# Two-layer encoder trunk: maxima exchanged behind the second transposes, edge pairs and norm sums placed later, last projection tile loaded four k-tiles at a time

## The chip, the cores and the metric

The kernel runs on one core of one Trainium2 chip. The metric is device time in microseconds of one execution; the kernel before has a median of 1507.74 us over 3 runs (1507.51 to 1507.95). PE is TensorE, DVE is VectorE, ACT is ScalarE, POOL is GpSimd and SP is SyncE, which issues nearly all DMAs. A "bank" is one of the eight 128x512 fp32 tiles of PSUM that the program allocates.

## What is computed

Input x is 1x512x1024 in fp32. Two layers, each a token mixer and an MLP, both behind an RMS norm and both added to the stream:

```python
h = h + mixer_a(rms_norm(h, norm1[0]), a_wqkv, q_gain, k_gain, a_wo, cos, sin)   # layer 0
h = h + mlp_sq_relu(rms_norm(h, norm2[0]), mlp_w1[0], mlp_w2[0])
h = h + mixer_b(rms_norm(h, norm1[1]), b_win, b_conv, b_wout)                    # layer 1
h = h + mlp_sq_relu(rms_norm(h, norm2[1]), mlp_w1[1], mlp_w2[1])
```

`mixer_a` is windowed attention of 16 heads of 64 columns in three groups (dilations 1, 4 and 16), each with its own q, k and v; q and k are normalised per head and partly rotated. The three groups share one softmax: their row maxima are compared, each group is weighted by exp(own maximum - greatest maximum), and numerators and denominators are added. `mixer_b` is a gated three-tap convolution between two projections. `mlp_sq_relu` is relu(h @ w1) squared, @ w2, with 4096 hidden columns.

## The kernel before

Every large product is three matmuls in fp32r: each fp32 operand is split into a high part and the rest (`wh`, `wl` for weights, `hgh`, `hgl` for activations), and high x high, high x rest and rest x high are added in PSUM (`add_unit`, matmul at L128). `split` (L288, L289) makes the parts: ACT casts the high one, DVE or, for weights, POOL subtracts for the rest.

The work of TensorE is a list of units in a fixed order: for each of the eight head pairs the columns q0, k0, q1 (unit A), k1, q2, k2 (unit B) and v; then the attention's output projection `wo`, the MLP, the convolution mixer and the second MLP. A position counts unit size: 1.0 is 16 matmuls of 384 columns or 12 of 512 columns. Everything else is a task with a position, held in a heap; `run_tasks` issues a task's instructions, on whatever engines, as soon as the matmul before its position has been issued. So an engine's order is set by the positions, and an instruction that waits holds up all behind it on its engine. `PLACES` has three sets of positions: for the first pair, for pairs 1 to 6, and for the last.

Weights come through `load_to` (DMA issue on SP into one of four `wraw` buffers) and `prep_to` (cast on ACT into `wh`, difference on POOL into `wl`, six buffers each), one k-tile of 128 rows at a time.

The pieces of a head pair, in their order (`attn_tasks`):

- The evacuations to `rawA` or `rawB`, the squares (`norm_sq`, L362), the inverse root (`norm_rs`, twelve small DVE instructions from L365 on: L151, L152, then three times L155 to L157) and the multiplication with the rotation (`norm_mul`, to L378).
- TA and TB: the first and second transposes (`qk_fill`, L387): four transposes of 128x128 fill a bank, ACT takes the high part from it (L401) and DVE the rest (L403). TA makes q0, k0, q1; TB makes k1, q2, k2.
- S0: scores of group 0 in two halves (L443), two banks each; DVE adds the mask and takes the maxima (L447). E0: the exponentials.
- X: the exchange of maxima. Group 0 has another row order than groups 1 and 2, so its maxima and sums are permuted: `spread` (L424, DVE), then at X + lX `stats_over`, which is `swap` (four small matmuls into one bank, L433) and a copy out of it (L478, DVE).
- S12: scores of groups 1 and 2 in four pieces (L457, one bank each, maxima L460), E12 their exponentials, W the weights of the groups (a second `swap`, copy L496), N0 and N12 the normalisation (L504 on DVE, L502 on POOL).
- PT: eight transposes of the probabilities (L516), split into `pth` and `ptl`; PV: the products with v (L544).

Banks: the projections take theirs from a pool of four (`psG`), the outputs have one (`psO`). TA, TB, S0, S12, `swap` and PT all take theirs in turn from one pool of three (`psT`), so each waits until the use three before it has been read out. `ident` is the identity matrix, the moving operand of a transpose.

After the last pair the output projection adds `xs` back (a DMA fetches it to `oT`, L768; L739 adds). `add_sums` has the sum of squares for the next norm split (`sgh`, `sgl`) and summed over the partitions by two matmuls with ones (L711, L712), and DVE then works out the inverse root `R` from it (L714 on).

The change touches `PLACES`, `add_unit` (a factor for its size), `add_sums`, and the unit of the last 128 columns of `wo` (L779).

Of the kernel before, what the change touches and what calls it, by code (L numbers as in the profile page):

```python
# [35 lines left out]
def _constants():  # L36
# [10 lines left out]
    for n, b in enumerate((0, 1, 3)):  # L47
# [10 lines left out]


PLACES = [  # L60
    dict(sqA=0.52, rsA=0.95, mulA=2.62, dmA=0.05, TA=6.3, dT=0.2, sqB=0.08, rsB=1.22, mulB=2.1, dmB=0.1, TB=6.2, S0=1.25,
         dS=0.65, E0=2.4, X=4.2, lX=1.3, S12=7.8, dS12=0.3, E12=8.4, dE12=0.2, W=10.0, lW=0.35, lF=0.9, N0=11.35, N12=10.45,
         dN=0.04, P=12.2, dP=0.6, gP=0.5, lP=1.6, qA=0, qB=0, pA=0, pB=3, pN=2, vA=0, vB=8, xq=2.7, dxq=0.3, xs=5.35,
         lg=2.48, dlg=0.36, tb=4.6, dtb=0.15, gc=6.7),
    dict(sqA=0.02, rsA=0.87, mulA=1.79, dmA=0.28, TA=4.8, dT=0.19, sqB=0.17, rsB=0.8, mulB=1.07, dmB=0.12, TB=4.05, S0=0.45,
         dS=0.55, E0=1.1, X=3.1, lX=1.3, S12=6.5, dS12=0.24, E12=7.1, dE12=0.2, W=8.9, lW=0.35, lF=0.9, N0=10.25, N12=9.4,
         dN=0.04, P=10.9, dP=0.64, gP=0.9, lP=1.6, qA=0, qB=0, pA=0, pB=3, pN=2, vA=0, vB=12),
    dict(sqA=0.02, rsA=0.87, mulA=1.79, dmA=0.28, TA=4.8, dT=0.19, sqB=0.17, rsB=0.8, mulB=1.07, dmB=0.12, TB=4.15, S0=0.45,
         dS=0.55, E0=1.1, X=3.1, lX=1.3, S12=6.5, dS12=0.24, E12=7.1, dE12=0.2, W=9.0, lW=0.4, lF=1.0, N0=10.5, N12=9.55,
         dN=0.04, P=11.1, dP=0.56, gP=0.45, lP=1.4, qA=0, qB=0, pA=0, pB=1, pN=2, vA=0, vB=9),  # L70
]


# [1 line left out]
def trunk_kernel(ctx, tc, x, norm1, norm2, wqkv, qgain, kgain, wo, win, conv, wout, w1, w2, c_rope, c_m0, c_m12, out):  # L75
    nc = tc.nc
    pe, act, dve, pool, sync = nc.tensor, nc.scalar, nc.vector, nc.gpsimd, nc.sync
    ctx.enter_context(tc.manual_schedule())

    def ptile(p, shape, dt, name, **kw):  # L80
        return p.tile(shape, dt, name=name, **kw)
# [26 lines left out]
    def close_pool(key):  # L108
        stacks.pop(key).close()

    def add_unit(cols, load, stat_mov, nb, alloc, width, done, begin=None, kblocks=((0, 1), (2, 3), (4, 5), (6, 7))):


        unit = {}
        ks = [k for b in kblocks for k in b]
        for i, blk in enumerate(kblocks):
            def emit(ws, blk=blk):
                if blk[0] == ks[0]:
                    if begin:
                        begin()  # L120
                    unit["ps"] = [alloc(n) for n in range(nb)]
                ops = []
                for n in range(nb):
                    for kt, (wh, wl) in zip(blk, ws):
                        prs = stat_mov(kt, wh, wl, n)
                        for q, (a, b) in enumerate(prs):
                            def mm(n=n, a=a, b=b, st=(kt == ks[0] and q == 0), sp=(kt == ks[-1] and q == len(prs) - 1)):
                                pe.matmul(unit["ps"][n][:, :width], a, b, start=st, stop=sp)  # L128
                                if sp:
                                    done(n, unit["ps"][n])  # L130
                            ops.append(mm)
# [9 lines left out]
    cols = ptile(const, [128, 64], F32, "cols")  # L141
# [127 lines left out]
    box = {}  # L269
# [149 lines left out]
    N0, D0, N0S, N12, D0S, D12, F0S, F12, NM, EX, F0 = 0, 1, 2, 3, 4, 5, 6, 7, 8, 9, 12  # L419
# [284 lines left out]
    def sums(pool_fn):  # L704
        hi = ptile(state["tp"], [128, S], R32, "sgh", tag="sgh", bufs=1)
        lo = ptile(state["tp"], [128, S], R32, "sgl", tag="sgl", bufs=1)
        split(hi, lo, state["sqa"])

        def mmf():
            ps = pool_fn(0)  # L710
            pe.matmul(ps, ones, hi, start=True, stop=False)  # L711
            pe.matmul(ps, ones, lo, start=False, stop=True)  # L712
            v = ptile(state["tp"], [128, S], F32, "nv", tag="nv", bufs=1)
            dve.tensor_scalar(out=v, in0=ps, scalar1=1.0 / D, scalar2=EPS, op0=ALU.mult, op1=ALU.add)  # L714
            rsqrt(state["R"], v, ptile(state["tp"], [128, S], F32, "zr"), ptile(state["tp"], [128, S], F32, "zz"))
        return mmf

    def add_sums(t0):
        box = {}
        at(t0 + 0.8, lambda: box.update(f=sums(ps_m)))  # L720
        at(t0 + 1.8, lambda: box["f"]())

    def ld_plain(w, c0, n=512):
        def f(raw, kt):
            sync.dma_start(raw[:, :n], w[128 * kt:128 * kt + 128, c0:c0 + n])
        return f
# [46 lines left out]
    sm_o = sm_T(lambda kt: hgA[kt])  # L773
# [2 lines left out]
    at(clock[0] - 2.0, lambda: split_o(KT - 1))  # L776
    at(clock[0] - 0.3, lambda: x_back(KT - 1))
    add_unit(384, ld_plain(wo[0], 512, 384), sm_o, 3, ps_w1, 512, lambda n, ps: wo_done(4 + n, ps), kblocks=((7,),))
    add_unit(128, ld_plain(wo[0], 896, 128), sm_o, 1, lambda n: ps_w1(3), 512, lambda n, ps: wo_done(7, ps))  # L779


    def open_mlp():
# [222 lines left out]
```

## Time and profile before

| | before |
|---|---|
| median of 3 runs | 1507.74 us (1507.51 to 1507.95) |
| the profiled execution: its own time | 1506.47 us |
| its span | 1504.7 us |
| mean granted clock of TensorE | 0.997 |
| PE busy | 1476.0 us (98%) |
| DVE, ACT, POOL busy | 714.8, 662.8, 702.5 us |
| chain that ended last | PE 90%, DVE 5%, issue 2%, ACT 1%, SPq 1% |

The span is the stretch from the first to the last instruction of the execution; 1.8 us of its own time lie around it. TensorE is busy nearly throughout, so the idle stretches of TensorE and the matmuls at half clock are the places at which time can be had. A busy share is modelled for matmuls, so the starts of two matmuls tell more than their lengths.

### The profile page before, as it was taken

The page shows a single profiled execution, that of the slowest core. Times are in us where ns is not written, and L with a number is a line of the kernel's source. Part 1 is how long each engine was busy: PE and PEld are TensorE (multiplying, and loading weights), DVE is VectorE, ACT ScalarE, POOL GpSimd, SP SyncE. Part 2 cuts the span into 40 slices and gives each one's busy share as a digit, 9 for nine tenths or more (in the row PEclk, how much of TensorE's full clock was granted, in tenths as well). Part 3 has the DMA queues.
Part 4 walks back from the last instruction along what each step waited for, and adds up shares of the span by engine and source line. Part 5 has one row for each costly group of instructions (what it writes and reads, how often), then busy time and mean ns, then how long its engine had stood idle before and what let it go on. Part 6 is the DMA issues. An engine that isn't in the chain of part 4 may idle for free.

```text
span 1504.7 us, 22546 instructions
## 1 busy us (share of the span) xinstructions
PE 1476.0 (98%) x7900; PEld 1289.6 (86%) x7900; DVE 714.8 (48%) x1464; ACT 662.8 (44%) x1364; POOL 702.5 (47%) x673
## 2 busy tenths in 40 slices
PE   9999999999999999999999999999999999999998
PEld 8899999999999987688888888878887888888887
DVE  6876667676767685743012223563447430122222
ACT  5555565565556563544333332433343443333320
POOL 4444444535444434554444445445455544444442
PEclk9999999999999999999999999999999999999999
DMA  6432322323132323333333332223333333333322
GB/s 168 127 106 77 89 80 81 97 64 113 53 114 63 103 73 115 117 99 98 99 98 96 93 100 95 84 79 111 95 107 98 99 98 98 99 96 94 99 91 84
DMA packets 164445, 144.76 MB, mean 96 GB/s; under 512 B 13876, under 2 KB 125292, under 8 KB 164332
## 3 DMA queue, kind: packets, MB, share of 16 engines
q1 hardware_dynamic: 164044, 143.06, 31.8%
q8 instruction: 62, 1.02, 0.3%
q14 instruction: 51, 0.42, 0.1%
q10 hardware_dynamic: 288, 0.27, 0.1%
HBM read 134.89 MB, written 8.39 MB: 95 GB/s over the span
## 4 chain that ended last, share of the span: by engine, by line
PE 90%; DVE 5%; issue 2%; ACT 1%; SPq 1%; DMA 0%; POOL 0%; POOLq 0%; ACTq 0%
PE g L128 82%; PE o L544 3%; PE st L516 2%; PE st L457 2%; PE st L387 1%; PE st L443 1%; DVE k1l L403 1%; ACT k1h L401 1%; DMA wraw<-in_a_wqkv 0%; POOL wl L289 0%; DVE sm L504 0%; ACT sqx L273 0%; SPq L567 0%; DVE sqa L698 0%; DVE tmpR L376 0%
## 5 line engine op out<-in xcount | busy, mean ns | idle before, releaser
L289 POOL TENSOR_TENSOR wl<-wraw,wh 128x512 fp32r<-128x512 f32 (+2 forms) x550 | 639.5, 1184 | 722.5 <-ACT wh L288 712.8
L288 ACT CAST wh<-wraw 128x512 fp32r<-128x512 f32 (+2 forms) x550 | 300.8, 564 | 502.0 <-PE g L128 389.2
L128 PE MATMUL g<-hgBh,wl 128*128 128x512 f32 x704 | 274.5, 390 | 1.9 <-POOL wl L289 1.9
L128 PE MATMUL g<-hgBh,wh 128*128 128x512 f32 x704 | 274.0, 389 | 0.0
L128 PE MATMUL g<-hgBl,wh 128*128 128x512 f32 x704 | 273.9, 389 | 0.0
L128 PE MATMUL g<-wh,hgl 128*128 128x384 f32 x768 | 267.7, 349 | 0.5 <-DVE hgl L302 0.3
L128 PE MATMUL g<-wl,hgh 128*128 128x384 f32 x768 | 262.0, 341 | 0.0
L128 PE MATMUL g<-wh,hgh 128*128 128x384 f32 x768 | 261.8, 341 | 0.0
L797 DVE SCALAR_TENSOR_TENSOR zr<-g,R 128x512 f32<-128x512 f32 x64 | 44.0, 691 | 285.1 <-PE g L128 284.9
L128 PEld LDWEIGHTS g<-hgBh,wl 128*128 128x128 f32 x704 | 132.1, 188 | 31.1 <-POOL wl L289 3.9
L128 PEld LDWEIGHTS g<-hgBh,wh 128*128 128x128 f32 x704 | 132.2, 188 | 27.7 <-ACT wh L288 0.4
L128 PEld LDWEIGHTS g<-hgBl,wh 128*128 128x128 f32 x704 | 132.2, 188 | 27.5
L128 PEld LDWEIGHTS g<-wh,hgl 128*128 128x128 f32 x768 | 145.1, 189 | 3.7 <-DVE hgl L302 1.6
L128 PEld LDWEIGHTS g<-wh,hgh 128*128 128x128 f32 x768 | 145.2, 189 | 0.3
L128 PEld LDWEIGHTS g<-wl,hgh 128*128 128x128 f32 x768 | 145.0, 189 | 0.3
L814 DVE TENSOR_TENSOR acc<-g,acc 128x512 f32<-128x512 f32 x32 | 22.1, 692 | 138.2 <-PE g L128 138.2
L128 PE MATMUL g<-z0h,wh 128*128 128x512 f32 x192 | 74.7, 389 | 0.0
L128 PE MATMUL g<-z0l,wh 128*128 128x512 f32 x192 | 74.7, 389 | 0.0
L128 PE MATMUL g<-z0h,wl 128*128 128x512 f32 x192 | 74.7, 389 | 0.0
L466 ACT ACTIVATE sm<-sm,mxs 128x256 f32<-128x256 f32 x128 | 63.6, 498 | 14.8 <-DVE mxs L460 11.2
L288 ACT CAST pth<-st 128x512 fp32r<-128x512 f32 x64 | 37.4, 584 | 66.2 <-PE st L516 64.9
L798 ACT ACTIVATE zz<-zr 128x512 f32<-128x512 f32 x64 | 40.4, 631 | 37.0 <-DVE zr L797 34.9
(212 smaller groups left out, 2353.8 us busy)
## 6 DMA issues: line engine op xcount, KB each, us to landing
wraw<-in_mlp_w SPq DMA_DIRECT2D x256, 256.0 KB
wraw<-in_a_wqkv SPq DMA_DIRECT2D x128, 128.0 KB
wraw<-in_a_wqkv SPq DMA_DIRECT2D x64, 192.0 KB
wraw<-in_a_wqkv SPq DMA_DIRECT2D x128, 64.0 KB
wraw<-in_b_win SPq DMA_DIRECT2D x64, 128.0 KB
v0d<-v SPq DMA_DIRECT2D x8, 512.0 KB
v<-v0d SPq DMA_DIRECT2D x64, 64.0 KB
wraw<-in_b_win SPq DMA_DIRECT2D x64, 64.0 KB
```

The costliest lines, as they stand in the source:

```text
L128: pe.matmul(unit["ps"][n][:, :width], a, b, start=st, stop=sp)
L288: act.copy(hi, src)
L289: (eng or dve).tensor_sub(lo, src, f32(hi))
L387: pe.transpose(o, raw[r][:, w, :], ident)
L401: act.activation(h_, v, AF.Copy, scale=sc)
L457: pe.matmul(pv[:, :, g], a[:, 128 * r:128 * r + 128], k[:, 256 * r:256 * r + 256], start=(q == 0), stop=(q == 2))
L466: act.activation(t[:, h, b], t[:, h, b], AF.Exp, bias=mx(m)[:, c], scale=-1.0, accum_out=mx(d)[:, c])
L516: pe.transpose(ps[:, 128 * n:128 * n + 128], src, ident)
L544: pe.matmul(out_, stat, mov, start=first and q == 0, stop=last and q == len(ops) - 1, skip_group_check=True)
L797: dve.scalar_tensor_tensor(zr, ps, 0.0, state["R"], op0=ALU.max, op1=ALU.mult)
L798: after(0.4, lambda: act.activation(zz, zr, AF.Square))
L814: dve.tensor_add(a, ps, a)
```

## The change

- **Exchange of maxima.** X + lX moves from 4.4 to 5.3 (pairs 1 to 6), from 5.5 to 7.1 (first pair) and from 4.4 to 5.9 (last pair), so that `swap` stands behind the k2 transposes and no longer between q2 and k2.
- **First pair.** TA from 6.3 to 7.0, S0 from 1.25 to 1.9, E0 and X with it.
- **Last pair.** TB from 4.15 to 4.7, S12 from 6.5 to 6.8, the weights and the normalisation 0.2 later, PT from 11.1 to 11.5.
- **Last tile of the output projection.** Its weights came in eight k-tiles of 128x128, each with a load, a cast on ACT and a difference on POOL; they now come four k-tiles at a time, as two loads and two pairs of 128x512. The 24 matmuls are the same.
- **Norm sums.** `add_sums` makes the split and the ones-matmuls 0.4 later (five matmuls) at its three places.

```diff
 PLACES = [
...
-         dS=0.55, E0=1.1, X=3.1, lX=1.3, S12=6.5, dS12=0.24, E12=7.1, dE12=0.2, W=8.9, lW=0.35, lF=0.9, N0=10.25, N12=9.4,
+         dS=0.55, E0=1.1, X=3.1, lX=2.2, S12=6.5, dS12=0.24, E12=7.1, dE12=0.2, W=8.9, lW=0.35, lF=0.9, N0=10.25, N12=9.4,
...
     def add_sums(t0):
         box = {}
-        at(t0 + 0.8, lambda: box.update(f=sums(ps_m)))
-        at(t0 + 1.8, lambda: box["f"]())
+        at(t0 + 1.2, lambda: box.update(f=sums(ps_m)))
+        at(t0 + 2.2, lambda: box["f"]())
...
-    add_unit(128, ld_plain(wo[0], 896, 128), sm_o, 1, lambda n: ps_w1(3), 512, lambda n, ps: wo_done(7, ps))
+    def ld_four(raw, i):
+        sync.dma_start(raw.rearrange("p (k n) -> p k n", k=4),
+                       wo[0][512 * i:512 * i + 512, 896:1024].rearrange("(k p) n -> p k n", p=128))
+
+    def sm_four(i, wh, wl, n):
+        return [pr for q in range(4) for pr in sm_o(4 * i + q, *(t[:, 128 * q:128 * q + 128] for t in (wh, wl)), 0)]
+
+    add_unit(512, ld_four, sm_four, 1, lambda n: ps_w1(3), 512, lambda n, ps: wo_done(7, ps), kblocks=((0,), (1,)), times=4)
```

`add_unit` takes `times` and multiplies the unit's size by it.

How the rows move. A row names line, operation, output and operands. On DVE, in each of pairs 1 to 6, from the rest of k1 (L403) to the first maxima of S12 (L460); L478 is the copy that empties the bank of `swap`, L292 makes the rest of v:

```order
 L403 SCALAR_TENSOR_TENSOR k1l<-st,cols,k1h 64x4x128 x2
 L403 SCALAR_TENSOR_TENSOR q2l<-st,cols,q2h 128x512
+L403 SCALAR_TENSOR_TENSOR k2l<-st,cols,k2h 64x4x128 x2
+L292 SCALAR_TENSOR_TENSOR v<-g,small,v 128x6x64 x2
 L478 COPY mxs<-st 128x2x8
-L403 SCALAR_TENSOR_TENSOR k2l<-st,cols,k2h 64x4x128 x2
-L292 SCALAR_TENSOR_TENSOR v<-g,small,v 128x6x64 x4
+L292 SCALAR_TENSOR_TENSOR v<-g,small,v 128x6x64 x2
 L460 ISA sm_131,mxs<-st,msk_107 128x256
 L460 ISA mxs 128x1
```

The copy has moved from ahead of k2's rest to behind it and two of the four v. TensorE's `swap` has moved with it, from ahead of the k2 transposes to 14 matmuls behind them.

On DVE in the first pair, behind the rest of k0 (L403): L362 are the last sums of squares of `rawB`, L365 begins the inverse root of `rawB` (its last rows are L156 and L157), L447 are the maxima of S0's first half:

```order
 L403 SCALAR_TENSOR_TENSOR k0l<-st,cols,k0h 128x448
 L403 SCALAR_TENSOR_TENSOR k0l<-st,cols,k0h 128x64
-L362 TENSOR_REDUCE stB<-sqq 128x6
-L403 SCALAR_TENSOR_TENSOR q1l<-st,cols,q1h 128x512
-L362 TENSOR_REDUCE stB<-sqq 128x6
-L447 ISA sm_130,mxs<-st,msk_106 128x256
-L447 ISA mxs 128x1
```

```order
 L156 SCALAR_TENSOR_TENSOR stB<-stB 128x24
 L157 SCALAR_TENSOR_TENSOR stB<-stB 128x24
+L403 SCALAR_TENSOR_TENSOR q1l<-st,cols,q1h 128x512
 L447 ISA sm_130,mxs<-st,msk_106 128x256
 L447 ISA mxs 128x1
```

The rest of q1, and the maxima behind it, have moved from ahead of the inverse root to behind it.

On DVE in the last pair, from the normalisation (L504, L496 between its halves) to the first rests of the transposed probabilities (L289 ptl); L739 are the sums that need a DMA of `xs`:

```order
 L504 TENSOR_SCALAR sm_131<-sm_131,mxs 128x256 x4
 L496 COPY mxs<-st 128x8
-L504 TENSOR_SCALAR sm_130<-sm_130,mxs 128x256 x3
 L739 TENSOR_TENSOR oT_78<-g,oT_78 128x512
-L504 TENSOR_SCALAR sm_130<-sm_130,mxs 128x256
+L504 TENSOR_SCALAR sm_130<-sm_130,mxs 128x256 x4
 L739 TENSOR_TENSOR oT_79<-g,oT_79 128x512
-L289 TENSOR_TENSOR ptl<-st,pth 128x512
 L739 TENSOR_TENSOR oT_80<-g,oT_80 128x512
-L289 TENSOR_TENSOR ptl<-st,pth 128x512 x4
+L289 TENSOR_TENSOR ptl<-st,pth 128x512 x5
```

One of the sums has moved ahead of three normalisations, and another (oT_80) ahead of the first `ptl`.

## Rows read from the trace of the kernel before

**Rows 1.** The page's busy time of each engine, over the span

```profile
PE 1476.0 (98%) x7900; PEld 1289.6 (86%) x7900; DVE 714.8 (48%) x1464; ACT 662.8 (44%) x1364; POOL 702.5 (47%) x673
```

**Rows 2.** Waits of TensorE: waiting tile and line, releaser: us in total, times, longest

```profile
PE st L387 <- DVE k1l L403: 9.8, 7, 1.4
PE st L387 <- DVE rawA L378: 3.5, 4, 1.6
PE g L128 <- POOL wl L289: 2.8, 5, 0.7
PE st L387 <- DVE rawB L378: 2.0, 2, 1.6
PE st L516 <- DVE sm L504: 1.4, 2, 0.9
```

**Rows 3.** Timeline of TensorE, pair 1 (start, us, instruction, count); chain of waits, one stretch

```profile
149.98 0.34 PE L128 MATMUL g<-wh,hgl 128*128 128x384 f32 x1
...
152.07 0.34 PE L128 MATMUL g<-wh,hgl 128*128 128x384 f32 x1
...
632.56 348.16 PE g L128 x1536
```

**Rows 4.** Timeline of pair 1 (idle before and its releaser in brackets)

```profile
137.16 0.26 PE L433 MATMUL st<-spread,fold 128*32 128x16 f32 x8
138.84 0.63 PE L387 MATMUL st<-ident,rawB 128*128 128x128 f32 x4 [1.43 <-DVE k1l L403]
...
137.18 1.51 DVE L403 SCALAR_TENSOR_TENSOR k1l<-st,cols,k1h 64x512 fp32r<-64x512 f32 x2 [2.33 <-ACT k1h L401]
140.92 1.51 DVE L403 SCALAR_TENSOR_TENSOR k2l<-st,cols,k2h 64x512 fp32r<-64x512 f32 x2 [1.36 <-ACT k2h L401]
146.12 0.42 DVE L460 CUSTOM_DVE_ANT_0 sm<-st,msk 128x256 f32<-128x256 f32 x1 [1.03 <-PE st L457]
```

**Rows 5.** First pair: timeline; windows (length, PE busy, clock, DMA share, GB/s)

```profile
52.13 0.47 PE L387 MATMUL st<-ident,rawA 128*128 128x128 f32 x1 [0.68 <-DVE rawA L378]
61.65 0.28 PE L443 MATMUL st<-k0h,q0l 64*128 64x256 f32 x2
...
55.65 0.88 DVE L403 SCALAR_TENSOR_TENSOR k0l<-st,cols,k0h 128x448 fp32r<-128x448 f32 x2 [1.07 <-ACT k0h L401]
57.31 0.75 DVE L403 SCALAR_TENSOR_TENSOR q1l<-st,cols,q1h 128x512 fp32r<-128x512 f32 x1 [0.33 <-ACT q1h L401]
60.51 1.02 DVE L365 SCALAR_TENSOR_TENSOR stB<-stB,small 128x24 f32<-128x24 f32 x1
63.73 0.18 DVE L157 SCALAR_TENSOR_TENSOR stB<-stB 128x24 f32<-128x24 f32 x1
...
52.20:56.60 4.40, 4.40 (x17) 0.50 0.35 97
```

**Rows 6.** Timeline of the last pair, TensorE and then DVE

```profile
550.12 0.33 PE L387 MATMUL st<-ident,rawB 128*128 128x128 f32 x1 [1.63 <-DVE rawB L378]
577.59 0.67 PE L516 MATMUL st<-ident,sm 128*128 128x128 f32 x3 [0.88 <-DVE sm L504]
582.93 0.28 PE L544 MATMUL o<-pth,v 128*128 128x256 f32 x1
...
582.41 0.69 DVE L739 TENSOR_TENSOR oT<-g,oT 128x512 f32<-128x512 f32 x1 [1.24 <-DMA oT<-xs]
```

**Rows 7.** Windows: busy PE, PEld, DVE, ACT, POOL, clock, DMA, GB/s; last `wo` tile

```profile
614.30:622.50 8.20, 4.96 (x16) 2.24 (x15) 7.50 (x10) 5.91 (x13) 6.44 (x6) 1.00 0.38 118
```

**Rows 8.** Timeline at the norm sums: convolution mixer first, then second MLP

```profile
981.21 0.69 DVE L714 TENSOR_SCALAR nv<-g 128x512 f32<-128x512 f32 x1 [2.58 <-PE g L712]
1000.71 0.50 PE L128 MATMUL g<-hgBh,wl 128*128 128x512 f32 x1 [0.44 <-POOL wl L289]
...
1157.43 0.49 PE L711 MATMUL g<-sgh,ones 128*128 128x512 f32 x1 [0.61 <-ACT sgh L288]
1158.15 0.50 PE L712 MATMUL g<-sgl,ones 128*128 128x512 f32 x1 [0.23 <-DVE sgl L289]
```

More of the change, by code (lines that the diff above doesn't have):

```diff
@@ L60 @@
 PLACES = [
-    dict(sqA=0.52, rsA=0.95, mulA=2.62, dmA=0.05, TA=6.3, dT=0.2, sqB=0.08, rsB=1.22, mulB=2.1, dmB=0.1, TB=6.2, S0=1.25,
-         dS=0.65, E0=2.4, X=4.2, lX=1.3, S12=7.8, dS12=0.3, E12=8.4, dE12=0.2, W=10.0, lW=0.35, lF=0.9, N0=11.35, N12=10.45,
+    dict(sqA=0.52, rsA=0.95, mulA=2.62, dmA=0.05, TA=7.0, dT=0.25, sqB=0.08, rsB=1.22, mulB=2.1, dmB=0.1, TB=6.2, S0=1.9,
+         dS=0.65, E0=3.05, X=4.9, lX=2.2, S12=7.8, dS12=0.3, E12=8.4, dE12=0.2, W=10.0, lW=0.35, lF=0.9, N0=11.35, N12=10.45,
          dN=0.04, P=12.2, dP=0.6, gP=0.5, lP=1.6, qA=0, qB=0, pA=0, pB=3, pN=2, vA=0, vB=8, xq=2.7, dxq=0.3, xs=5.35,
@@ L65 @@
     dict(sqA=0.02, rsA=0.87, mulA=1.79, dmA=0.28, TA=4.8, dT=0.19, sqB=0.17, rsB=0.8, mulB=1.07, dmB=0.12, TB=4.05, S0=0.45,
-         dS=0.55, E0=1.1, X=3.1, lX=1.3, S12=6.5, dS12=0.24, E12=7.1, dE12=0.2, W=8.9, lW=0.35, lF=0.9, N0=10.25, N12=9.4,
+         dS=0.55, E0=1.1, X=3.1, lX=2.2, S12=6.5, dS12=0.24, E12=7.1, dE12=0.2, W=8.9, lW=0.35, lF=0.9, N0=10.25, N12=9.4,
          dN=0.04, P=10.9, dP=0.64, gP=0.9, lP=1.6, qA=0, qB=0, pA=0, pB=3, pN=2, vA=0, vB=12),
-    dict(sqA=0.02, rsA=0.87, mulA=1.79, dmA=0.28, TA=4.8, dT=0.19, sqB=0.17, rsB=0.8, mulB=1.07, dmB=0.12, TB=4.15, S0=0.45,
-         dS=0.55, E0=1.1, X=3.1, lX=1.3, S12=6.5, dS12=0.24, E12=7.1, dE12=0.2, W=9.0, lW=0.4, lF=1.0, N0=10.5, N12=9.55,
-         dN=0.04, P=11.1, dP=0.56, gP=0.45, lP=1.4, qA=0, qB=0, pA=0, pB=1, pN=2, vA=0, vB=9),
+    dict(sqA=0.02, rsA=0.87, mulA=1.79, dmA=0.28, TA=4.8, dT=0.19, sqB=0.17, rsB=0.8, mulB=1.07, dmB=0.12, TB=4.7, S0=0.45,
+         dS=0.55, E0=1.1, X=3.1, lX=2.8, S12=6.8, dS12=0.24, E12=7.4, dE12=0.2, W=9.2, lW=0.4, lF=1.0, N0=10.7, N12=9.75,
+         dN=0.04, P=11.5, dP=0.54, gP=0.45, lP=1.4, qA=0, qB=0, pA=0, pB=1, pN=2, vA=0, vB=9),
 ]
@@ L109, in close_pool, with add_unit @@
         stacks.pop(key).close()
-    def add_unit(cols, load, stat_mov, nb, alloc, width, done, begin=None, kblocks=((0, 1), (2, 3), (4, 5), (6, 7))):
+    def add_unit(cols, load, stat_mov, nb, alloc, width, done, begin=None, kblocks=((0, 1), (2, 3), (4, 5), (6, 7)), times=1):
         unit = {}
@@ L132, in emit @@
                 return ops
-            size = len(blk) * nb * width / 2048.0
+            size = len(blk) * nb * width * times / 2048.0
             blocks.append(dict(first=len(loads), n=len(blk), emit=emit, start=clock[0], size=size))
```

## The prediction

> **What bounds the kernel.** I read the page's busy times first: TensorE is busy for 98% of the span, DVE, ACT and POOL for under half of it [rows 1]. So the time is the matmuls plus what TensorE loses, and the change leaves the matmuls as they are. The list of TensorE's waits names the losses: transposes (L387) that wait for `k1l`, 9.8 us in 7 waits, more transposes for `rawA` (3.5) and `rawB` (2.0), transposes of probabilities for `sm` (1.4) and matmuls for `wl` (2.8) [rows 2]. Last I read the timeline at each of these places, to see what the wait hangs on. Two prices serve throughout: from 149.98 to 152.07 twelve matmuls of 384 columns start, 0.174 us each, and 1536 matmuls of 512 columns take 348.16 us, 0.227 us each [rows 3]. I count by starts, as the lengths of matmuls overlap.
>
> **Term 1, pairs 1 to 6: 8.6 us.** In pair 1 the k2 transposes wait 1.43 us for `k1l` [rows 4]. They don't read it: three banks go round, k1, q2, `swap`, k2 take one each, so k2 needs the bank of k1, which DVE's `k1l` empties at 137.18 + 1.51 = 138.69, just ahead of their start at 138.84. With `swap` behind k2, the k2 transposes take the bank before that of k1, which the scores S0 had and which has long been read. The wait goes, in all six pairs (the list's longest is 1.4, and of its 9.8 the last pair has 1.2): 6 x 1.43 = 8.6. What is late next? `swap` itself now needs k1's bank. It stands 14 matmuls (2.4 us) behind k2's transposes, at about 137.4 + 2.4 = 139.8, after 138.69. S12's first piece needs q2's bank and `k2l`: `k2l` ended at 142.43 and will end some 1.4 earlier, while DVE waits 1.03 us for S12 before its first maxima at 146.12 [rows 4], so S12 is set by TensorE's own order. Its third piece needs the bank of `swap`, emptied by L478, now behind `k2l` and two v: about 141.0 + 2 x 0.6 + 0.2 = 142.4 against a need near 144.5. Nothing in the second half of a pair waits today, so the gain stays. Bounds 8.4 and 9.0, which is 0.03 less and 0.07 more for each wait.
>
> **Term 2, first pair: 1.3 us.** Waits for `rawA` are 3.5 us [rows 2], and the stretch 52.20 to 56.60 ran at a granted clock of 0.50, that is 1.2 GHz, after TensorE had stood idle between the transposes [rows 5]; the same matmuls need about half of those 4.40 us at 2.4 GHz, so about 2.1 us are lost beside the waits. The first transposes come twelve matmuls (2.09 us) later, so they find more of `rawA` ready, but its last part still comes at 52.1 [rows 5]. Then DVE sets the pace: the rest of q1 now stands behind the inverse root of `rawB`, twelve instructions that took from 60.51 to 63.91, 3.4 us [rows 5]. From the end of `k0l` (56.5) that is 56.5 + 3.4 + 0.75 = 60.7 for q1's bank, and two maxima on 61.4 for the other bank that S0's second half needs. Its twelve matmuls take about 1.0, so it ends near 62.4, where it ended at 61.93 before, with ten matmuls (1.74) more behind it: 1.74 - 0.5 = 1.3. Bounds: -0.2, if POOL's work stretches that chain by 1.5; 3.6, if the chain is hidden and the clock holds (1.3 + 2.1 + 0.2). The trace shows the low clock behind the idle stretch; the Trainium skill, page "TensorE: Matmul & The Clock Gate", section "What's actually happening", says that the throttled state is the default and that activity releases it. By that rule fewer stalls would give all of those 2.1 back; the sum doesn't use it, since S0 waits for DVE at either clock.
>
> **Term 3, last pair: 1.0 us.** Waits are 2.0 for `rawB`, 1.2 for `k1l` (9.8 - 8.6) and 1.4 for `sm` [rows 2], and transposes move back behind nine matmuls (1.56). But only 0.88 of one wait at 577.59 and 1.63 of another at 550.12 stand on their own [rows 6]; the chain `rawB`, `k1l`, maxima, normalisation is made by DVE, ACT and POOL, and starts from `rawB` as before. I put the first transposes of probabilities 1.3 us earlier with five matmuls more behind them. The gain is then checked by the next thing: the first `ptl` now stands behind the sum of oT_80, which waited for its DMA until 582.41 [rows 6]. The first PV needs `ptl`; it started at 582.93, and will start between 582.5 and 583.4 with four matmuls (0.91) more ahead of it. So 0.9 + 0.4 down to 0.9 - 0.5; I take 1.0, nearer the upper one, as the DMA's issue moves forward with TensorE. Bounds 0 and 4.5 (all waits less 0.1).
>
> **Term 4, last tile: 4.0 us.** From 614.30 to 622.50 fourteen matmuls start (x16 in the row counts the two at its edges), which need 14 x 0.227 = 3.2 us of the 8.2: 5.0 are lost, at busy DVE, ACT and POOL (7.50, 5.91, 6.44 of 8.2) [rows 7]. Eight casts and eight differences of 128x128 become two and two of 128x512, and the loads of the MLP begin earlier, as fewer buffers are held. I leave 1.0 for what POOL still owes there and for the sums of the first MLP, which come just in time. Bounds 2.0 and 5.0. The Trainium skill, same page, section "Back-to-back issue gap", gives about 131 ns for a sustained matmul of 512 columns; by that the fourteen need 1.8 us and the place would be worth 6.4. The trace doesn't agree, with 227 ns over 1536 of them, and decides.
>
> **Term 5, sums of the convolution mixer: -1.1 us.** Here no matmul waited for the sums; DVE waited 2.58 us for the ones-matmuls [rows 8], so five matmuls later (1.13 us) is 1.13 later for `R` and all behind it, up to the weights' casts on ACT behind an activation that waits for DVE. Matmuls already wait 0.44 for `wl` at 1000.71 [rows 8]; that wait grows by 1.1. Bounds -1.6 (two such matmuls) and 0 (the cover is longer than this row says).
>
> **Term 6, sums of the second MLP: 1.1 us.** The first of the ones-matmuls waits 0.61, and the second starts 0.72 behind it, where 0.227 is the pace [rows 8]: 0.61 + 0.49 = 1.1 are lost. The split's inputs come as before, and 1.13 more matmul time lies ahead of the ones: 1.1. Bounds 0.5 and 1.3. The first MLP's are in term 4.
>
> **The sum.** 8.6 + 1.3 + 1.0 + 4.0 - 1.1 + 1.1 = 14.9 us. The profiled execution took 1506.47, 1.27 below the median of the runs, so 1491.6 for it; against the median, 1507.74 - 14.9 = **1492.8**.
>
> **The rivals.**
>
> - *All edge waits vanish*: 9.0 + 3.6 + 4.5 + 5.0 + 0 + 1.3 = 23.4, 1484.3 us. For it: the edge waits are each under 2 us and the moves are 1 to 2 us. Against it: the chains of the first and last pair run on DVE, which the change loads earlier. Chance 0.12.
> - *Edge stalls move on*: S0's second half, the first PV and the MLP's sums wait for as much as was saved. 8.4 - 0.2 + 0 + 2.0 - 1.6 + 0.5 = 9.1, 1498.6 us. For it: the moved rows of DVE. Chance 0.17.
> - *The six waits only move*: the banks don't go round as I read them, or the k2 transposes wait for `rawB` or ACT instead. 14.9 - 8.6 = 6.3, 1501.4 us. This is the change that doesn't do what it says. Against it: 138.69 and 138.84 fit the round of three. Chance 0.06.
> - *Slower: the copy of the exchange holds a bank.* L478 stands behind two v on DVE, and the third piece of S12 in each of six pairs needs its bank. It has 2.1 us of slack by the working above. If the v's wait for their matmuls and the copy comes 2.1 + d late, the six pairs lose 6 d, and the kernel is slower than before by over 0.2% from d = (14.9 + 3.0) / 6 = 3.0: at d = 3.2 the time is 1492.8 + 19.2 = 1512.0 us. Against it: the v's were evacuated right behind `k2l`, without a wait. Chance 0.03.
>
> **How the numbers follow.** My forecast has 0.62, the rivals 0.12, 0.17, 0.06 and 0.03. The range leaves out the ends: half of the first rival, the last two, and a tail of my own; it reaches from 1486.5 (the sum with the upper bounds of the terms 2 and 3) to 1499.0 (the second rival). A measurement can tell about 0.2%, 3 us, from no change. All but the last rival are faster by more; I keep 0.05 for a gain of under 3 us, if terms 1 and 4 both fall, and 0.02 for slower.
>
> **What would show it right or wrong.** Term 1: no wait for `k1l` in pairs 1 to 6, and nothing in its place at `swap` or S12's third piece; the list of waits should lose 8.6 there. Term 2: S0's second half waits for DVE's maxima near 61, and the low clock may stay. Term 3: the first PV waits for `ptl` behind the sum of oT_80. Term 4: a loss of about 1 us where 5.0 were. Terms 5 and 6: a longer wait for `wl` some 20 us behind the convolution's sums, none at the second MLP's. A wait for `k1l` or S12's bank in each pair would make the prediction wrong.

## The result and the profile after

The changed kernel takes 1490.75 us (median of 5 runs, 1490.09 to 1491.70), the kernel before 1507.51 us (5 runs): the ratio is 0.9889, with a 95% interval of 0.9875 to 0.9904. That is 16.8 us less, where 14.9 were forecast; 1492.8 was predicted, in a range of 1486.5 to 1499.0. The profiled execution took 1490.46 us with a span of 1488.7 us; between the two profiled executions the difference is 16.0 us.

The page's first line and the list of TensorE's waits of the changed kernel (columns as in [rows 1, 2]). Lines up to L776 have the numbers they had before:

```profile
PE 1474.2 (99%) x7900; PEld 1289.7 (87%) x7900; DVE 714.4 (48%) x1464; ACT 660.8 (44%) x1358; POOL 700.6 (47%) x667
```

```profile
PE st L387 <- DVE rawB L378: 2.0, 1, 2.0
PE st L387 <- DVE rawA L378: 1.9, 3, 0.8
PE st L516 <- DVE sm L504: 1.4, 1, 1.4
...
PE g L128 <- DVE v L292: 0.8, 1, 0.8
PE g L128 <- POOL wl L289: 0.4, 1, 0.4
PE st L443 <- DVE mxs L447: 0.3, 1, 0.3
...
PE st L443 <- DVE q1l L403: 0.2, 1, 0.2
```

All seven waits for `k1l` are gone, and of the 2.8 us for `wl` 0.4 are left. The waits for `rawB` and `sm` are as long as before, and three are new: `v`, `mxs` and `q1l`.

To see what each part gave, I set the start of every projection matmul (L128; their order is the same in both kernels) of the one trace against its start in the other, and read the difference at points where both have settled:

| up to the matmul that started at (before, after) | gain so far | of this stretch | forecast |
|---|---|---|---|
| 11.16, 10.88 (start of the kernel) | 0.28 | 0.3 | 0 |
| 78.09, 76.44 (first pair) | 1.64 | 1.4 | 1.3 |
| 485.07, 474.94 (pairs 1 to 6) | 10.13 | 8.5 | 8.6 |
| 602.89, 592.40 (last pair) | 10.49 | 0.4 | 1.0 |
| 633.53, 618.13 (last tile, sums of the first MLP) | 15.40 | 4.9 | 4.0 |
| 996.24, 981.31 (sums of the convolution mixer) | 14.93 | -0.5 | -1.1 |
| 1159.65, 1143.56 (sums of the second MLP) | 16.09 | 1.2 | 1.1 |

**Pairs 1 to 6.** Timeline of pair 1 after, TensorE and then DVE; it answers to [rows 4]:

```profile
135.53 0.60 PE L387 MATMUL st<-ident,rawB 128*128 128x128 f32 x4
138.49 0.26 PE L433 MATMUL st<-spread,fold 128*32 128x16 f32 x8
144.90 0.28 PE L457 MATMUL st<-k1h,q1h 128*128 128x256 f32 x1
...
135.65 1.51 DVE L403 SCALAR_TENSOR_TENSOR k1l<-st,cols,k1h 64x512 fp32r<-64x512 f32 x2 [2.33 <-ACT k1h L401]
137.86 1.50 DVE L403 SCALAR_TENSOR_TENSOR k2l<-st,cols,k2h 64x512 fp32r<-64x512 f32 x2
139.40 1.14 DVE L292 SCALAR_TENSOR_TENSOR v<-g,small,v 128x384 fp32r<-128x384 f32 x2
140.46 0.16 DVE L478 COPY mxs<-st 128x16 f32<-128x16 f32 x1
143.16 0.42 DVE L460 CUSTOM_DVE_ANT_0 sm<-st,msk 128x256 f32<-128x256 f32 x1 [1.04 <-PE st L457]
```

The k2 transposes start at 135.53, before `k1l` has even begun, and have no wait in brackets. `swap` follows at 138.49, after `k1l`'s end at 137.16. The copy ends at 140.62, and the third piece of S12, which needs its bank, begins at 144.90. DVE still waits 1.04 us for S12.

**First pair.** Timeline after, TensorE and then DVE, and one window; it answers to [rows 5]:

```profile
60.46 0.38 PE L443 MATMUL st<-k0h,q0h 64*128 64x256 f32 x1 [0.21 <-DVE q1l L403]
61.73 0.39 PE L443 MATMUL st<-k0h,q0l 64*128 64x256 f32 x2
...
56.64 0.93 DVE L151 TENSOR_SCALAR stB<-stB 128x24 int32<-128x24 int32 x1
57.60 0.18 DVE L152 TENSOR_SCALAR stB<-stB 128x24 int32<-128x24 int32 x1
...
59.66 0.74 DVE L403 SCALAR_TENSOR_TENSOR q1l<-st,cols,q1h 128x512 fp32r<-128x512 f32 x1
```

```profile
52.00:56.40 4.40, 4.40 (x19) 0.64 0.33 90
```

S0's second half waits for `q1l`, which stands behind the inverse root (L151 and L152 are its second and third row), and 0.3 us for the maxima behind that; it ends at 62.1. The granted clock of 52.00 to 56.40 is 0.64: 1.2 GHz for most of it.

**Last pair.** Timeline after, TensorE and then DVE; it answers to [rows 6]:

```profile
541.48 0.33 PE L387 MATMUL st<-ident,rawB 128*128 128x128 f32 x1 [2.00 <-DVE rawB L378]
567.96 0.30 PE L516 MATMUL st<-ident,sm 128*128 128x128 f32 x1 [1.41 <-DVE sm L504]
573.37 0.28 PE L544 MATMUL o<-pth,v 128*128 128x256 f32 x1
...
566.86 0.69 DVE L739 TENSOR_TENSOR oT<-g,oT 128x512 f32<-128x512 f32 x1 [2.55 <-DMA oT<-xs]
571.62 0.69 DVE L739 TENSOR_TENSOR oT<-g,oT 128x512 f32<-128x512 f32 x1 [0.95 <-DMA oT<-xs]
```

`rawB` is waited for as long as before. The first PV has no wait, but the first transposes of probabilities do: DVE stood idle 2.55 us for the DMA of the first sum (oT_78), and the normalisations that the transposes need stood behind it.

**Last tile and sums.** Window over the last matmuls of the last tile and the first of the MLP (columns as in [rows 7]), then weight loads (PEld) behind the convolution mixer's sums and the ones-matmuls of the second MLP; they answer to [rows 7, 8]:

```profile
602.91:607.22 4.31, 4.31 (x21) 3.45 (x19) 4.31 (x8) 3.15 (x6) 0.18 (x1) 1.00 0.13 47
```

```profile
980.35 0.19 PEld L128 LDWEIGHTS g<-hgBh,wl 128*128 128x128 f32 x1 [0.49 <-POOL wl L289]
981.31 0.19 PEld L128 LDWEIGHTS g<-hgBh,wl 128*128 128x128 f32 x1 [0.44 <-POOL wl L289]
...
985.78 0.50 PE L128 MATMUL g<-hgBh,wl 128*128 128x512 f32 x1 [0.44 <-POOL wl L289]
...
1142.86 0.39 PE L711 MATMUL g<-sgh,ones 128*128 128x512 f32 x1
1143.22 0.50 PE L712 MATMUL g<-sgl,ones 128*128 128x512 f32 x1
```

TensorE is busy throughout this stretch, and POOL, busy 6.44 of 8.2 us before, for 0.18 of 4.31. Behind the convolution's sums two weight loads wait for `wl`: the first didn't before, the second waited 0.31 us (at 996.24 of the trace before). The old wait of 0.44, now at 985.78, has stayed what it was. The ones-matmuls of the second MLP wait no more.

### The profile page after: what moved, and what is told of

It is laid out like the page before. It is cut to its first block, busy times and chain, and to the rows that moved or that the text cites. A ratio compares the mean times of both kernels' runs of the same rounds, so it can differ in the third digit from the quotient of the medians.

```text
span 1488.7 us, 22510 instructions
## 1 busy us (share of the span) xinstructions
PE 1474.2 (99%) x7900; PEld 1289.7 (87%) x7900; DVE 714.4 (48%) x1464; ACT 660.8 (44%) x1358; POOL 700.6 (47%) x667
## 4 chain that ended last, share of the span: by engine, by line
PE 92%; DVE 4%; issue 1%; DMA 1%; ACT 1%; SPq 1%; POOL 0%; POOLq 0%; DVEq 0%; ACTq 0%
PE g L128 84%; PE o L544 3%; PE st L516 2%; PE st L457 2%; PE st L387 1%; PE st L443 1%; DMA sm<-in_x 0%; POOL wl L289 0%; SPq L567 0%; ACT sqx L273 0%; DVE tmpR L376 0%; DMA oT<-xs 0%; DVE rawB L371 0%; PE g L869 0%; DMA wraw<-in_a_wqkv 0%
## 5 line engine op out<-in xcount | busy, mean ns | idle before, releaser
L289 POOL TENSOR_TENSOR wl<-wraw,wh 128x512 fp32r<-128x512 f32 (+1 forms) x544 | 637.6, 1194 | 707.9 <-ACT wh L288 695.2
L288 ACT CAST wh<-wraw 128x512 fp32r<-128x512 f32 (+1 forms) x544 | 299.7, 568 | 501.1 <-PE g L128 378.5
L128 PE MATMUL g<-hgBh,wl 128*128 128x512 f32 x704 | 274.5, 390 | 0.5 <-POOL wl L289 0.4
L128 PE MATMUL g<-hgBh,wh 128*128 128x512 f32 x704 | 274.1, 389 | 0.1
L128 PE MATMUL g<-hgBl,wh 128*128 128x512 f32 x704 | 274.0, 389 | 0.0
L128 PE MATMUL g<-wh,hgl 128*128 128x384 f32 x768 | 267.7, 349 | 0.4 <-DVE hgl L302 0.3
L128 PE MATMUL g<-wl,hgh 128*128 128x384 f32 x768 | 262.5, 342 | 0.0
L128 PE MATMUL g<-wh,hgh 128*128 128x384 f32 x768 | 262.1, 341 | 0.0
L128 PEld LDWEIGHTS g<-hgBh,wl 128*128 128x128 f32 x704 | 132.1, 188 | 29.4 <-POOL wl L289 2.3
L128 PEld LDWEIGHTS g<-hgBh,wh 128*128 128x128 f32 x704 | 132.1, 188 | 27.8 <-ACT wh L288 0.5
L128 PEld LDWEIGHTS g<-hgBl,wh 128*128 128x128 f32 x704 | 132.1, 188 | 27.6
L128 PEld LDWEIGHTS g<-wh,hgl 128*128 128x128 f32 x768 | 145.0, 189 | 3.8 <-DVE hgl L302 1.6
L128 PEld LDWEIGHTS g<-wh,hgh 128*128 128x128 f32 x768 | 145.3, 189 | 0.4 <-DVE rawB L323 0.2
L128 PEld LDWEIGHTS g<-wl,hgh 128*128 128x128 f32 x768 | 145.0, 189 | 0.4
L128 PE MATMUL g<-z0l,wh 128*128 128x512 f32 x192 | 74.7, 389 | 0.0
L128 PE MATMUL g<-z0h,wl 128*128 128x512 f32 x192 | 74.7, 389 | 0.0
L128 PE MATMUL g<-z0h,wh 128*128 128x512 f32 x192 | 74.7, 389 | 0.0
```

## The experiments

Theory: three banks in a round explain the six waits, and the remaining gain comes from the last tile; at the edges DVE's order decides, so that most moves there only shift a wait. The rival for each part stands with its run.

**1. The exchange alone.** The kernel before, with one number changed:

```diff
-         dS=0.55, E0=1.1, X=3.1, lX=1.3, S12=6.5, ... W=8.9, ...
+         dS=0.55, E0=1.1, X=3.1, lX=2.2, S12=6.5, ... W=8.9, ...
```

> The kernel before with one edit: in pairs 1 to 6 the exchange of maxima stands behind the k2 transposes (lX 2.2). Theory (three banks go round; k2 had to wait for k1's bank): the six waits of 1.43 us for k1l go, nothing takes their place, 8.5 us less, about 1499.0. Rival (the gain of these pairs rests on the other moves too, or is given back later): less than half of it, above 1503.

Measured: 1498.47 us (4 runs, 1497.97 to 1498.56) against 1507.23, ratio 0.9945 (0.9928 to 0.9961). The six waits are gone. This one number gives 8.8 us, a little over half of the change.

**2 and 3. Where in the round it stands.** The changed kernel, with the exchange between the k1 and q2 transposes, and with the exchange ahead of k1:

```diff
-         dS=0.55, E0=1.1, X=3.1, lX=2.2, S12=6.5, ... W=8.9, ...
+         dS=0.55, E0=1.1, X=3.1, lX=1.05, S12=6.5, ... W=8.9, ...
```

```diff
-         dS=0.55, E0=1.1, X=3.1, lX=2.2, S12=6.5, ... W=8.9, ...
+         dS=0.55, E0=1.1, X=3.1, lX=0.85, S12=6.5, ... W=8.9, ...
```

> The changed kernel, but in pairs 1 to 6 the exchange stands between the k1 and the q2 transposes (lX 1.05). Theory (banks go round by threes: k1, exchange, q2, then k2 on k1's bank again): the wait of 1.43 us for k1l is back in front of k2 in each of six pairs, 8.5 us more than the changed kernel, about 1499. Rival (what hurt was the small matmuls and the copy standing between q2 and k2, or TensorE coming too early): no wait, 1490 to 1491.

> The changed kernel, but in pairs 1 to 6 the exchange stands one matmul ahead of the k1 transposes (lX 0.85), earlier than in the kernel before. Theory (round of three banks): k2 takes the bank of the exchange, which its copy empties ahead of k1l; no wait for k1l, within 1 us of the changed kernel, 1490 to 1491.5. Rival (the exchange has to come later, for itself or for DVE): the waits are back, about 1499 or more.

Measured: 1499.46 us for the first, in one run. Its list of waits, and TensorE's timeline in pair 1:

```profile
PE st L387 <- DVE k1l L403: 7.4, 6, 1.2
```

```profile
134.62 0.26 PE L433 MATMUL st<-spread,fold 128*32 128x16 f32 x8
135.09 0.60 PE L387 MATMUL st<-ident,rawB 128*128 128x128 f32 x4
137.45 0.63 PE L387 MATMUL st<-ident,rawB 128*128 128x128 f32 x4 [1.23 <-DVE k1l L403]
```

`swap` no longer stands between q2 and k2, yet k2 waits for k1's bank again, in each of the six pairs. The second took 1494.13 us, in one run; the same view of it:

```profile
135.75 0.26 PE L433 MATMUL st<-spread,fold 128*32 128x16 f32 x8
136.22 0.60 PE L387 MATMUL st<-ident,rawB 128*128 128x128 f32 x4
137.18 0.60 PE L387 MATMUL st<-ident,rawB 128*128 128x128 f32 x4
138.15 0.60 PE L387 MATMUL st<-ident,rawB 128*128 128x128 f32 x4
```

Here the exchange is earlier than it ever was, and nothing waits for `k1l`. So it is the place in the round of three that counts, not earlier or later: anything that takes one bank beside q2 between k1 and k2 makes k2 wait for k1. The expected time was missed by 2.6 us: by the comparison of matmuls with the changed kernel 2.3 us were lost in the first pair and before, which the edit doesn't touch, and 1.6 in pairs 1 to 6, where two matmuls now wait for v, 1.0 us in all. Behind the transposes is the better place of the two that fit.

**4. The fetch of xs.** The changed kernel, with the DMAs for the last three residual sums issued earlier:

```diff
-        at(clock[0] + (9.0 + k if k < 4 else 3.2 + 0.7 * (k - 4)), lambda k=k: x_back(k))
+        at(clock[0] + (9.0 + k if k < 4 else 2.2 + 0.5 * (k - 4)), lambda k=k: x_back(k))
```

> The changed kernel, but the DMAs that fetch the last three xs tiles for the residual sums are issued at 2.2, 2.7 and 3.2 of the projection instead of 3.2, 3.9 and 4.6. Theory: in the last pair DVE stands idle 2.55 us for the first of these DMAs ahead of the last four normalisations, and the first transposes of probabilities wait 1.41 us for them; with the DMA earlier that wait goes, 1 to 1.5 us less than the changed kernel, about 1489.3. Rival (the normalisation is set by the chain from rawB, or the PV behind it by ptl): the wait only moves, less than 0.4 us.

Measured: 1491.01 us, in one run, where 1489.3 were expected. DVE's timeline in the last pair:

```profile
566.10 0.68 DVE L739 TENSOR_TENSOR oT<-g,oT 128x512 f32<-128x512 f32 x1
```

The sum waits for no DMA, and TensorE's wait for `sm` falls from 1.4 to 0.3 us: the cause is shown. By the comparison of matmuls this place gives 1.3 us (the loss of this run against the changed kernel goes from 1.84 to 0.53 there). The whole time doesn't show it, for two losses that the edit doesn't touch. Up to the end of the first pair 1.3 us were lost: the clock was 1.00 from 52.00 to 56.40, so TensorE came earlier to the wait for `q1l`, and the clock fell behind that wait. TensorE's timeline, and a window (columns as in [rows 5]):

```profile
60.16 0.38 PE L443 MATMUL st<-k0h,q0h 64*128 64x256 f32 x1 [1.44 <-DVE q1l L403]
```

```profile
62.00:66.00 4.00, 4.00 (x15) 0.57 0.02 4
```

And behind the 2.0 us wait for `rawB` the clock fell too, where the changed kernel's trace has 1.00 (run 12 shows that row). Here is the window of the 5 us behind the wait in run 4:

```profile
542.84:547.84 5.00, 5.00 (x23) 0.66 0.25 88
```

This cost 1.6 us, of which 1.1 came back, as the wait for `v` behind it fell away.

**5. The last tile alone.** The kernel before, with the new functions and the unit of the last tile as in the change:

```diff
-    add_unit(128, ld_plain(wo[0], 896, 128), sm_o, 1, lambda n: ps_w1(3), 512, lambda n, ps: wo_done(7, ps))
+    add_unit(512, ld_four, sm_four, 1, lambda n: ps_w1(3), 512, lambda n, ps: wo_done(7, ps), kblocks=((0,), (1,)), times=4)
```

> The kernel before with one edit: the last 128 columns of the output projection come as two loads of four k-tiles, two casts and two differences. Theory (eight small sets of casts and differences held TensorE at this place, 5.0 us): from the start of that tile to the first matmuls of the MLP 4 to 5 us less, the waits for wl and wh there gone, about 1502.8. Rival (the place is bound by the loads of the MLP's weights or by the residual sums on DVE): under 2 us less.

Measured: 1504.41 us, in one run, against 1508.19 (one run too). By the comparison of matmuls the tile and the MLP's first matmuls gain 5.0 us, and then 1.0 is lost at the sums of the first MLP, which stand at their old place in this kernel. The whole time is no measure of this: the last pair, which the edit doesn't touch, was 2.0 us longer than in the trace before, at a granted clock of 0.58 in the 5 us behind its wait for `rawB`. TensorE's timeline at the sums:

```profile
629.95 0.50 PE L712 MATMUL g<-sgl,ones 128*128 128x512 f32 x1 [0.52 <-DVE sgl L289]
```

So at the first MLP the later sums protect what the tile gives: 4.0 us without them, 4.9 with them.

**6. The convolution's sums at their old place.** The changed kernel with

```diff
-    add_sums(clock[0] + 2.0)
+    add_sums(clock[0] + 1.6)
     for j in range(KT):
```

> The changed kernel with the norm sums of the convolution mixer back at their old place (0.4 earlier there, the other two places as changed). Theory (no matmul waited for these sums, and R comes later with them): the stretch from the ones-matmuls to 30 us behind them is 0.4 to 1.1 us shorter. Rival (R has slack, the 0.44 us wait for wl behind it has another cause): the stretch is the same within 0.1 us.

Measured: the stretch is 0.5 us shorter (the loss of this run against the changed kernel goes from 2.32 to 1.85 there), so `R` comes later by the change and that costs 0.5; the wait of 0.45 behind it stays. Five matmuls are 1.13 us, and DVE does begin on the sums (L714) 1.14 us earlier in this run, measured against the matmuls; but its chain from there to L905 takes 10.97 us, and 10.30 in the changed kernel. One of its rows in this run, and the same row in the changed kernel:

```profile
969.78 1.45 DVE L155 TENSOR_TENSOR zz<-R 128x512 f32<-128x512 f32 x1
```

```profile
969.39 0.69 DVE L155 TENSOR_TENSOR zz<-R 128x512 f32<-128x512 f32 x1
```

In this run, as in the kernel before, POOL makes `wl` beside this row and the next one (1.39 us in place of 0.69); in the changed kernel POOL has finished by then, and the row beside it is L152 (1.12 us in place of 0.43). The time of the one run, 1492.27 us, is longer for what happened in the first pair above all (2.0 us), which the edit doesn't touch.

**7. Rotations of the last pair on POOL.** The changed kernel with

```diff
-         dN=0.04, P=11.5, dP=0.54, gP=0.45, lP=1.4, qA=0, qB=0, pA=0, pB=1, pN=2, vA=0, vB=9),
+         dN=0.04, P=11.5, dP=0.54, gP=0.45, lP=1.4, qA=0, qB=0, pA=0, pB=3, pN=2, vA=0, vB=9),
```

> The changed kernel, but in the last pair POOL rotates three of the four row groups of rawB, as in the other pairs, instead of one (pB 3). Theory (the wait of 2.0 us for rawB is set by DVE, whose rotations take 1.0 us in place of 0.65 and 0.95 in place of 0.34 while POOL makes wl): the wait for rawB falls below 0.7, and the next waits (v, sm) take back at most half, 0.5 to 1.5 us less. Rival (rawB is late because of its inputs, or POOL is then late with wl): the wait for rawB stays at 1.5 or more, or a wait for wl takes its place.

Measured: 1493.17 us, in one run, 2.4 more than the changed kernel. The wait for `rawB` is gone, as expected, but neither side foresaw what came in its place: `swap` waits 2.18 us for `k1l`, and the clock behind that is 0.50 (549 to 552). ACT's timeline, then TensorE's:

```profile
540.87 0.52 ACT L288 CAST wh<-wraw 128x384 fp32r<-128x384 f32 x1 [5.77 <-PE st L387]
542.04 0.52 ACT L288 CAST wh<-wraw 128x384 fp32r<-128x384 f32 x1 [0.65 <-DMA wraw<-in_a_wo]
...
543.10 1.38 ACT L401 ACTIVATE k1h<-st,cols 64x512 fp32r<-64x512 f32 x2
```

```profile
546.18 0.22 PE L433 MATMUL st<-spread,fold 128*32 128x16 f32 x3 [2.18 <-DVE k1l L403]
```

The k1 transposes had been done since 539.8; ACT had three casts in front of them: one that began only at 540.87, one that waited for weights of the output projection, and one of `hgh`. Here the next limit was close behind.

**8 to 11. A version that beats both.** Run 8 places the first pair's pieces later still; run 9 adds to it the edits of runs 4 and 6 and moves one evacuation to ACT; run 10 adds two edits to the last pair; run 11 is run 9 with DVE's order changed:

```diff
 # run 8
-    dict(..., TA=7.0, ..., S0=1.9, ..., E0=3.05, X=4.9, lX=2.2, ...)
+    dict(..., TA=8.0, ..., S0=2.9, ..., E0=4.05, X=5.9, lX=1.7, ...)
 # run 9, first pair as well
-    vA=0, vB=8
+    vA=0, vB=0
 # run 10, last pair
-    pB=1
+    pB=2
-        split(*hgA[k], oT[k])
+        split(*hgA[k], oT[k], eng=pool if k < 3 else dve)
 # run 11, first pair, on top of run 9
-    rsB=1.22, mulB=2.1
+    rsB=2.95, mulB=3.7
```

> The changed kernel, but in the first pair the first transposes and the scores of group 0 come 1.0 later still (TA 8.0, S0 2.9, E0 4.05, exchange at 5.9 and 7.6). Theory (DVE's order sets the second half of S0: the rest of q1 behind the inverse root): the inverse root now comes ahead of all of the transposes' rests, S0 waits for nothing, rawA's waits of 1.9 us go and with them the half clock behind them: 2 to 4.5 us less up to the end of the first pair. Rival (the waits only move: k2, S12 or the exchange of the first pair become late): under 1 us less.

> The changed kernel with three edits together: the convolution's norm sums at their old place, the last three xs fetches a unit earlier, and in the first pair the positions of the run p0_late with the last evacuation of rawB on ACT in place of DVE (it held a projection bank for 3.0 us there). Theory (each wait named in the traces of the single edits is real and the edits don't collide): 0.5 for the sums, 0.5 to 1 for the normalisation behind the xs fetch, 1.5 to 2.5 in the first pair: about 1487.5, 2 to 4 us less than the changed kernel. Rival (stalls at the edges only change their place): 1490 to 1492.

> As best_a, and in the last pair POOL rotates two of the four row groups of rawB (pB 2) and makes the rests of the first three projection inputs (hgl), which DVE made between the rests of k1, q2, k2 and v. Theory (DVE sets the pace of the last pair): waits for rawB and v, 2.8 us in the changed kernel, fall below 1.0, about 1.5 us less than best_a, 1486. Rival (ACT's casts that wait for the projection weights, or POOL, set it, as in the run with three rotations on POOL): the wait moves to k1l, the same as best_a or more.

> As best_a, but in the first pair the inverse root of rawB and its multiplications stand behind the rests of q0, k0, q1 and the maxima of S0's first half (rsB 2.95, mulB 3.7). Theory (the order of DVE alone sets the end of the first pair; in best_a the inverse root ahead of the rests of q0 and k0 cost 4.2 us of waits at S0): the waits for q0l and k0l go, TensorE leaves the first pair 4 to 5 us earlier than in best_a, about 1486.5, 4 us less than the changed kernel. Rival (what DVE has to do up to k1 is the bound in any order): the wait appears at k1's transposes as one for rawB or at S0's second half, 1489.5 or more.

Measured: 1490.77 us in run 8 (one run), 1491.27 in run 9 (4 runs, ratio 0.9892, 0.9876 to 0.9909), 1490.80 in run 10 (4 runs, 0.9888, 0.9873 to 0.9902), 1485.60 in run 11 (5 runs, 1484.35 to 1486.18, ratio 0.9853, 0.9839 to 0.9866). TensorE's timeline of run 8:

```profile
52.92 0.44 PE L128 MATMUL g<-wh,hgh 128*128 128x384 f32 x1 [2.96 <-DVE rawB L323]
```

Of run 9:

```profile
59.50 0.55 PE L443 MATMUL st<-k0h,q0h 64*128 64x256 f32 x1 [3.04 <-DVE q0l L403]
61.22 0.55 PE L443 MATMUL st<-k0h,q0h 64*128 64x256 f32 x1 [1.17 <-DVE k0l L403]
```

Of run 11:

```profile
57.79 0.35 PE L443 MATMUL st<-k0h,q0h 64*128 64x256 f32 x1 [0.18 <-DVE k0l L403]
```

In run 8 the wait for `rawA` turned into one for an evacuation of rawB on DVE, which stood behind the multiplications of rawA and held a projection bank. In run 9 that is gone too. TensorE reached the last projection matmul ahead of S0 at 56.13, the changed kernel reached the same matmul at 63.02, with all of S0 behind it; in run 9 S0 then waited 4.2 us, since the inverse root of rawB stood ahead of the rests of q0 and k0, and ran at a granted clock of 0.50 (60 to 64). At the end of the first pair run 9 was 1.9 us later than the changed kernel; further on its other two edits gave 1.3 and 0.5, as in runs 4 and 6. Only when the inverse root had been put behind those rests did the gain stay: in run 11 S0 waits 0.18, the granted clock is 1.00 both from 52.00 to 56.40 and from 62 to 66, the first pair is 4.1 us shorter than in the changed kernel, and the kernel is 21.8 us faster than the one before. The later placements of runs 8 and 9 were worth nothing without this last edit; whether the last edit needs them was not run. In run 10, in the last pair, the waits for `rawB` went, but one for `k1l` (1.6) came, and that for `v` grew from 0.8 to 1.3.

**12. The last pair as before.** The changed kernel with the last dict of `PLACES` as it was.

> The changed kernel with the last pair's positions as they were before. The comparison of the two traces by matmul puts the moves of the last pair at 0.4 us, where the prediction had 1.0. Theory (the waits of the last pair only change their place): the stretch of the last pair, from its scores of group 0 to the last tile of the projection, is within 1 us of the changed kernel, and the time 1490.5 to 1492.0. Rival (the moves matter, and something else lost their gain in the changed kernel's trace): 1 to 3 us more than the changed kernel, 1492.0 to 1494.

Measured: 1493.28 us (4 runs, 1491.06 to 1494.79, ratio 0.9903, 0.9886 to 0.9919), 2.5 more than the changed kernel and in the range of the rival, though the intervals overlap. The trace has the last pair 2.3 us longer. Window of this run over the 5 us behind its last wait for `rawB` (columns as in [rows 5]), and below it of the changed kernel:

```profile
540.70:545.70 5.00, 4.70 (x26) 0.58 0.12 39
```

```profile
541.48:546.48 5.00, 5.00 (x38) 1.00 0.26 88
```

The clock fell in this execution and not in that one. With the same old positions it fell in runs 1 and 5 too (0.66 and 0.58), and not in the trace of the kernel before (1.00). So the moves of the last pair are worth 0.4 us where the clock holds in both, as the comparison of matmuls says; whether they are worth more because the clock falls less often with them, as the medians suggest, stays open (of the traces with such a wait, it fell in 4 of 8 with the new positions, and in 3 of 4 with the old).

## Why the prediction was right, and where its sizes were off

- **Term 1 was right in mechanism and size**: 8.5 us by matmuls, 8.8 in run 1, 8.6 forecast. Runs 2 and 3 show the round of three. The slower rival, the copy behind two v, has its place in the trace: the copy ends at 140.62, 4.3 us before the third piece of S12, where the working left it 2.1. The k1l wait of the last pair went too, but there something else held the pair.
- **Term 2 was right in mechanism, and in size for this execution**: 1.4 us for 1.3, and by the steps named: the forecast had the rest of q1 ready at 60.7 and S0's second half end at 62.4, the trace has 60.40 and 62.1. The low clock stayed (0.64). The size is luck in part. The first pair is the same in runs 2, 3, 4, 6, 7 and 12. In the traces of 2, 7 and 12, with the low clock from 52.00 to 56.40 as here, it gained 0.9 to 1.4 us against the trace before. In 3, 4 and 6 the clock was 1.00 there, TensorE only came earlier to the same wait, 1.4 us for `q1l`, and had 0.57 from 62 to 66: these gained -0.3 to 0.0, as little as the lower bound of -0.2. (The trace before is one execution too: in run 1 the old first pair took 1.0 us more.) The sum priced the end of S0 at either clock, but not a fall of the clock behind it. So the 2.1 us that the half clock costs weren't to be had by this change; run 11, without the waits, has the full clock in both stretches. The rule of the Trainium skill, page "TensorE: Matmul & The Clock Gate", section "What's actually happening", that activity releases the throttle, agrees with that trace.
- **Term 3 was off**: 0.4 us for 1.0, inside its bounds. The step that failed is "The first PV needs `ptl`": I followed the sum of oT_80 ahead of `ptl`, and not that of oT_78, which the same listing shows ahead of three normalisations. That one had the longer DMA wait (2.55 us) and held up the transposes themselves (1.41 us, run 4). Also, `rawB` did not stay where it was: the transpose that waits for it comes 1.5 us later against the gain so far (541.48, where 550.12 - 10.13 = 539.99). The last two steps of its rotation took 1.03 and 0.93 us on DVE while POOL made differences for the next weights, and 0.36 and 0.26 before.
- **Term 4 was too small**: 4.9 us for 4.0. The 1.0 that I left for POOL and for the first MLP's sums was not needed: POOL works 0.18 of 4.31 us there, and the sums, also later, have no wait. Run 5 shows that it is the sums' move that keeps the last 1.0. The stretch that I called the last tile ends with five matmuls of the MLP (from 619.47); the 5.0 lost there were read rightly.
- **Term 5 had the right mechanism**, and was too large: -0.5 for -1.1. Weight loads wait for `wl` because ACT's casts stand behind an activation that waits for DVE, as the step said. The step that failed is "1.13 later for `R`": the sums came 1.13 later, but the chain behind them ran 0.67 us shorter, because less of it fell beside POOL's differences (run 6). And the wait of 0.44, on which I put the price, has another cause, as run 6 shows.
- **Term 6 was right**: 1.2 for 1.1.

Against the sum of 14.9 the profiled executions differ by 16.0: +0.9 in term 4, +0.6 in term 5, -0.6 in term 3, and 0.3 at the kernel's start. That terms 3 and 5 cancel is luck. The lower end of the range has a slip: by the sum given for it, it is 1487.0 and not 1486.5.

## What to carry to other kernels

When pieces share a small round of buffers, count which use takes which buffer: one small use put between two large ones can make the second wait for the first. What counts is its place in the round: behind the k2 transposes it cost nothing here, between k1 and q2 the wait was back, and ahead of k1 the wait was gone again. For a move on an engine that runs in order, list everything that the moved instruction passes, DMA-waiting sums above all, and price each on the consumer nearest to it. At the edges of a schedule try moves together: here the later placements in the first pair gave nothing in runs 8 and 9, and 4.1 us when the last wait had gone.

## What the runs showed of the hardware

- The clock falls behind short idle stretches of TensorE in some executions and not in others. Behind the same 2.0 us wait for `rawB` the granted clock of the next 5 us was 1.00 in the changed kernel and in runs 3, 8 and 9, and 0.66 in runs 2, 4, 6 and 11 (the two levels are 1.00, 2.4 GHz, and 0.50, 1.2 GHz). In runs 4 and 6 the fall cost 1.6 us, of which 1.1 came back, as the wait for `v` behind it fell away. With the old positions the last pair lost 2.0 us in run 5 and 2.3 in run 12, and 0.3 in run 1.
- Several of DVE's instructions are stretched while POOL makes `wl`. In the changed kernel the L378 of the last pair took 0.93 us beside POOL, and L151 of the first pair 0.93 where L152 behind it took 0.18. The first of these rows:

```profile
540.50 0.93 DVE L378 TENSOR_TENSOR rawB<-tmpR 128x96 f32<-128x96 f32 x1
```

  In the first pair of the same trace, with POOL idle, L378 took 0.26. The Trainium skill, page "SBUF — State Buffer", section "Who interferes with whom", says that a DVE instruction with two inputs in SBUF contends with a POOL instruction that reads SBUF; L378 has two such inputs, and the trace agrees. L151 has one, and that sentence doesn't cover it.
